# A table of expert products and weights: blocks of two experts by two tokens in place of rows of experts

## The chip, the cores and the metric

The kernel runs on one core of one Trainium2 chip. The metric is the device time of one execution in microseconds (us). TensorE is PE (its weight loads are PEld), VectorE is DVE, ScalarE is ACT, GpSimd is POOL, and SyncE (SP) issues most DMAs.

## The reference, cut to what matters

One transformer-like block on 256 tokens of width 2048: adaLN, a gated MLP and a retention mixer, and then a PEER layer, which is the part that the change touches:

```python
sc = jnp.einsum('thpd,hpnd->thpn', q, subkeys)      # 8 heads, 2 halves, 128 keys
v1, i1 = lax.top_k(sc[:, :, 0], 16); v2, i2 = lax.top_k(sc[:, :, 1], 16)
...                                                 # the 16 best of 16 x 16 sums
eidx = i1 * 128 + i2 (chosen pairs); gate = softmax(top)
a = jnp.einsum('td,thkd->thk', xt, emb_u[eidx])     # 128 chosen experts per token
w = gelu(a) * gate
y = jnp.einsum('thk,thkd->td', w, emb_v[eidx])
```

There are 16,384 experts, 128 chosen for each token.

## The kernel before, in words

The kernel doesn't gather whole expert rows. 768 of the 2048 columns of `emb_u` are gathered by expert (the dots of L762), and for the other 1280 columns PE multiplies **all** experts with all tokens. The results go into one table in SBUF, `A` (L915), of 128 partitions by 128 by 256 fp32 words. An expert is `i1 * 128 + i2`: `n` (the middle index) is `i1`, the partition is `i2`, and `t` is the token. So `A[:, n, t]` lies at word `256 n + t` of a partition: the 256 tokens of one `n` are adjacent, and two neighbours in `n` are 1 KB apart.

Four stages touch `A`:

- **The products** (loop at L919): PE forms 128 x 256 blocks in PSUM (`u_products`), and after every fourth half of an `n` pair ACT copies two `n` at once into `A` (L923, 64 copies of 512 words).
- **The routing stage** (loop at L1024, 32 units of 8 tokens). For a unit, `one_hot` (L948) builds two sets of one-hot matrices, `o1` from `i1` and `o2` from `i2`, on DVE, ACT and POOL (L954, L957, L958, L960); the letters of `ON1`, `ON2`, `ON3` and the counts of `SHARE1`, `SHARE2` say who builds which. `turned` (L965) transposes `o2` on PE (L971) and copies it out of PSUM on ACT (L972). `pick` (L975) multiplies, token by token, the turned `o2` (stationary) with that token's column block of `A` (moving, L981); each of these fp32 products is issued as two passes. DVE then takes the word of the right `n` with one masked sum for each token (`jk`, L985). `weight` (L988) adds the gathered part, applies gelu on ACT (L991) and the gate on DVE (L992). `scatter` (L994) runs two units later: POOL multiplies `o1` by the weights (L997), PE forms the 128 x 128 table of weights of each token (L1001, two passes each), and ACT copies four tokens at a time from PSUM over the picked columns of `A` (L1002). In the first half of the units POOL and DVE also finish the last 16 gathered dots (L755, L762).
- **The second products** (loop at L1137, 128 steps): `v_load(i)` takes row `n = i` of `A`, which now holds weights, splits it into `wh` (ACT, L1075) and `wl` (DVE, L1077), splits the row block of `emb_v` that a DMA brought into `vh` and `vl` (L1079, L1081), and PE accumulates over the steps (L1131). POOL gathers the other 576 columns of `emb_v`, two gathers a step, and DVE adds them (L1064).
- **The end**: `A` is reused as plain memory, `spent` (L1084), for the residual.

Each engine runs its instructions in order, and an instruction of one engine waits for those of others. The calls of `pick`, `turned` and `scatter` are interleaved by hand by unit (`LEAD`, `LAG`, `AHEAD1`); PE's order of a unit is pick, turned of the next unit, scatter of two units back. The number of buffers sets how far an engine runs ahead: three for `o1`, five for `o2`, four for the turned copies.

The lines that read or write the table:

```python
nc.scalar.copy(A[:, n // 2 - 1:n // 2 + 1], sums.pop(n // 4))                      # L923
mm = nc.tensor.matmul(pkv[:, t], oh[:, t], A[:, :, t0 + t], start=True, stop=True)  # L981
put = nc.scalar.copy(A[:, :, t0 + h:t0 + h + 4].rearrange("p n t -> p t n"), pwv)   # L1002
nc.scalar.copy(wh, W[:, i])                                                         # L1075
nc.vector.tensor_tensor(wl, W[:, i], wh.bitcast(F32), op=ALU.subtract)              # L1077
```

Of the kernel before, what the change touches and what calls it, by code (L numbers as in the profile page):

```python
# [10 lines left out]
F32 = mybir.dt.float32  # L11
# [5 lines left out]
ALU = mybir.AluOpType  # L17
# [4 lines left out]
P = 128  # L22
T = 256
# [9 lines left out]
NK = 128  # L33
# [81 lines left out]
def block_kernel(ctx, tc, a, out):  # L115
    nc = tc.nc
    def pool(name, side, bufs=1, space=None):
        stack = ExitStack()
        kw = {} if space == bass.MemoryType.DRAM else {"reuse_waits": "tile"}
        if space is not None:  # L120
            kw["space"] = space
        return stack.enter_context(tc.tile_pool(name=name, bufs=bufs, side=side, **kw)), stack
# [642 lines left out]
    def dot(tt, n, early=False, after=None):  # L765
        if early:
            g = gather(late["pg"], "eg", u_rows, UG, EG, tt, n)
        else:
            g = gather(ph, "hT", u_rows, UG, 8, tt, n, after)
        times(g, tt, n)  # L770
# [106 lines left out]
    def columns():  # L877
        softmax()
        nc.scalar.copy(idr, ident)
        for dst, src in ((i1T, i12[:, 0]), (i2T, i12[:, 1]), (gT, gate)):  # L880
            pt = bank("pt")
            for tt in range(TT):
                nc.tensor.transpose(pt[:, tt * P:(tt + 1) * P], src[:, tt], ident)
            nc.scalar.copy(dst, pt[:, :T])
            if dst is i2T:
                nc.scalar.mul(neg, pt[:, :T], -1.0)
# [4 lines left out]
    sums = {}  # L891

    def u_products(n):
        for m in range(n + len(ready), min(n + 2, 2 * NK)):
            ready.append(u_load(m))
        hi, lo = ready.pop(0)
        first, last = n % 2 == 0, n % 2 == 1
        if n % 4 == 0:
            sums[n // 4] = bank("mmu").rearrange("p (b t) -> p b t", b=2) if n // 4 % 2 else pm.tile([P, 2, T], F32, tag="mm", name="mmu")
        acc = sums[n // 4][:, n // 2 % 2]  # L900
        k0, k1 = HALF[n % 2]
        steps = ((hi, 0), (hi, 1), (lo, 0)) if n >= DIRECT else ((hi, None),)
        for i, (w, part) in enumerate(steps):
            for k in range(k0, k1):
                x = late["x1T"][:, UK + k] if part is None else h2T.op(part, UK + k)
                mm = nc.tensor.matmul(acc, w[:, k - k0], x, start=(first and k == 0 and i == 0),  # L906
                                      stop=(last and k == FK - 1 and i == len(steps) - 1))
        return mm

    for n in range(DIRECT):  # L910
        mm = u_products(n)
    late["pg_s"].close()
    st_s.close()
    big, big_s = pool("big", "left")
    A = big.tile([P, NK, T], F32, tag="big", name="A")  # L915

    rate = (len(todo) - LEFT) / (2 * NK - PRE)
    done = 0
    for n in range(2 * NK):  # L919
        if n >= DIRECT:  # L920
            mm = u_products(n)
        if n % 4 == 3:
            nc.scalar.copy(A[:, n // 2 - 1:n // 2 + 1], sums.pop(n // 4))  # L923
        if n == COLS:
            columns()
        while done < rate * (n + 1 - PRE):
            dot(*todo.pop(0), after=mm)
            done += 1
# [10 lines left out]
    def psum(tag, bufs):  # L939
        b = pq.tile([P, 512], F32, tag=tag, bufs=bufs, name=tag)  # L940
        return b, b.rearrange("p (t n) -> p t n", t=4)
# [33 lines left out]
    def pick(u):  # L975
        for h in range(2):
            t0 = u * SET + 4 * h
            oh = ohs.pop((u, h))
            pk, pkv = psum("pk", 3)
            for t in range(4):  # L980
                mm = nc.tensor.matmul(pkv[:, t], oh[:, t], A[:, :, t0 + t], start=True, stop=True)  # L981
                tc.declare_no_dep(mm.ins, group="scattered", reason="other tokens' columns")
            for t in range(4):
                jk = p2.tile([P, P], F32, tag="jk", bufs=2, name="jk")
                nc.vector.scalar_tensor_tensor(jk, iota, i1T[:, t0 + t:t0 + t + 1], pkv[:, t],  # L985
                                               op0=ALU.is_equal, op1=ALU.mult, accum_out=wT[:, t0 + t:t0 + t + 1])
# [7 lines left out]
    def scatter(u):  # L994
        t0 = u * SET
        o1, o2 = o1s.pop(u), o2s.pop(u)
        nc.gpsimd.tensor_tensor(o1, o1, wT[:, t0:t0 + SET, None].to_broadcast([P, SET, P]), op=ALU.mult)  # L997
        for h in range(0, SET, 4):
            pw, pwv = psum("pw", 3)
            for t in range(4):  # L1000
                nc.tensor.matmul(pwv[:, t], o2[:, h + t].bitcast(F32), o1[:, h + t], start=True, stop=True)  # L1001
            put = nc.scalar.copy(A[:, :, t0 + h:t0 + h + 4].rearrange("p n t -> p t n"), pwv)  # L1002
            tc.add_to_no_dep_group("scattered", put.ins)

    units = T // SET
# [18 lines left out]
    for u in range(-LEAD, units + LAG):  # L1024
        if 0 <= u < units and u % half == 0:
            tt = u // half
            while tt and fetched:
                last_dot()
            pt, _ = psum("pk", 3)
            nc.tensor.transpose(pt[:, :P], wrow[:, tt], ident)  # L1030
            nc.vector.tensor_copy(agT[:, tt * P:(tt + 1) * P], pt[:, :P])
        if 0 <= u < units:
            pick(u)
            weight(u)
        if u + LEAD < units:
            o2s[u + LEAD] = one_hot(1, u + LEAD, (ON2 if u * SET < T // 2 else ON3)[u % 4])
            turned(u + LEAD)
        if 0 <= u < half and fetched and (u + 1) * LEFT > took * half:
            last_dot()
        if u >= LAG:  # L1040
            scatter(u - LAG)
        if 0 <= u + 1 - LAG + AHEAD1 < units:
            v = u + 1 - LAG + AHEAD1
            o1s[v] = one_hot(0, v, ON1[v % 4])
        if 0 <= u < units and u % half == half - 1:
            pt, _ = psum("pk", 3)
            nc.tensor.transpose(pt[:, :P], wT[:, tt * P:(tt + 1) * P], ident)
            nc.vector.tensor_copy(wrow[:, tt], pt[:, :P])
    W = A

    p2_s.close()
    pq_s.close()
    py, py_s = pool("py", "left", bufs=1, space=PSUM)
# [16 lines left out]
    def v_load(i):  # L1070
        room, bufs = (p3, 1) if i % 3 == 2 else (pv, 2)
        vb = room.tile([P, GV], F32, tag="vb", bufs=bufs, name="vb")
        nc.sync.dma_start(vb, v_cols[i * P:(i + 1) * P])
        wh = p3.tile([P, T], F32R, tag="wh", bufs=3, name="wh")
        nc.scalar.copy(wh, W[:, i])  # L1075
        wl = p3.tile([P, T], F32R, tag="wl", bufs=3, name="wl")
        nc.vector.tensor_tensor(wl, W[:, i], wh.bitcast(F32), op=ALU.subtract)  # L1077
        vh = p3.tile([P, GV], F32R, tag="vh", bufs=2, name="vh")
        nc.scalar.copy(vh, vb)  # L1079
        vl = p3.tile([P, GV], F32R, tag="vl", bufs=2, name="vl")  # L1080
        late["split"] = nc.vector.tensor_tensor(vl, vb, vh.bitcast(F32), op=ALU.subtract)  # L1081
        return vh, vl, wh, wl

    spent = A.rearrange("p n t -> p (n t)")  # L1084
    x1 = spent[:, :TT * D].rearrange("p (t d) -> p t d", t=TT)
    xo = spent[:, TT * D:2 * TT * D].rearrange("p (t d) -> p t d", t=TT)
    ga2, gf = spent[:, 4 * D:5 * D], spent[:, 5 * D:6 * D]
# [39 lines left out]
    def product(i, ops, j, tt, n):  # L1127
        vh, vl, wh, wl = ops
        l, r = ((wh, vh), (wl, vh), (wh, vl))[j]
        c, w = chunks[n]  # L1130
        return nc.tensor.matmul(yp[tt][n][:, :w], l[:, tt * P:(tt + 1) * P], r[:, c:c + w],  # L1131
                                start=(i == 0 and j == 0), stop=(i == NK - 1 and j == 2))

    nxt = v_load(0)
    nc.scalar.sqrt(rf, late["ssum"])
    done, rate = 0, len(todo) / (NK - ENDS)
    for i in range(NK - 2):  # L1137
        ops = nxt
        nxt = v_load(i + 1)
        for j in range(3):  # L1140
            for tt in range(TT):
                for n in range(len(chunks)):
                    mm = product(i, ops, j, tt, n)
        while todo and done < rate * (i + 1):
            weigh(*todo.pop(0), after=mm)
            done += 1
        if i == BACK:
            restore(mm)
    ends = [nxt, v_load(NK - 1)]
    for tt in range(TT):  # L1150
        residual(tt, len(parts) - 1)
# [62 lines left out]
```

## Time and profile before

| | us |
|---|---|
| median of 3 runs (2393.7 to 2401.22) | 2394.3 |
| span of the profiled execution, first to last instruction | 2393.9 |
| PE busy | 2208.9 |
| DVE busy | 1785.1 |
| ACT busy | 1031.0 |
| POOL busy | 874.9 |

The profiled execution's span lies 0.4 us under the median. A share of busy time is a mean over stages with different limits, so the stages are read one by one: the routing stage lies from about 1600 to 1804 us of the span, the products before it, the second products after it, to 2365 us.

### The profile page before, as it was taken

How to read it: one execution, taken by the hardware profiler on the slowest of the kernel's cores; microseconds unless marked ns; L12 is line 12 of the kernel's file. 1: busy time of each engine (PE TensorE's matmuls, PEld its weight loads, DVE VectorE, ACT ScalarE, POOL GpSimd, SP SyncE). 2: the span in 40 equal slices, each digit the busy share in tenths (PEclk: the TensorE clock that was granted, in tenths of full speed). 3: DMA queues.
4: the chain of work that ended last, by engine and by line, in shares of the span. 5: the costliest groups of instructions: out<-in, count | busy, mean ns of one | idle time of the engine just before them, and what ended most of it. 6: DMA issues, size and time to landing. Idle time of an engine off the chain costs nothing. (4 is left out here: it accounts for less than half of the span.)

```text
span 2393.9 us, 37307 instructions
## 1 busy us (share of the span) xinstructions
PE 2208.9 (92%) x13988; PEld 1949.2 (81%) x13988; DVE 1785.1 (75%) x3416; ACT 1031.0 (43%) x1440; POOL 874.9 (37%) x750
## 2 busy tenths in 40 slices
PE   6999999999999998893999999989998998998996
PEld 3577779999999888783889999989997777777775
DVE  3478878888788755787767777777766877877777
ACT  3245556643344444101444444457774333333333
POOL 0000000000000002766444444467775665666664
PEclk9999999999999999996999999999999999999998
DMA  9977778777777765767999999971107888888987
GB/s 353 380 296 265 273 267 297 276 286 283 285 295 282 264 213 180 257 224 221 302 302 313 318 316 313 305 248 54 33 1 253 310 301 297 304 306 299 313 310 269
DMA packets 144312, 638.26 MB, mean 267 GB/s; under 512 B 20721, under 2 KB 26625, under 8 KB 112001
## 3 DMA queue, kind: packets, MB, share of 16 engines
q1 hardware_dynamic: 102146, 459.65, 53.7%
q0 software_dynamic: 41984, 176.23, 21.8%
q8 instruction: 109, 1.79, 0.3%
q14 instruction: 73, 0.60, 0.1%
HBM read 631.59 MB, written 4.20 MB: 266 GB/s over the span
## 5 line engine op out<-in xcount | busy, mean ns | idle before, releaser
L755 POOL DMA_INDIRECT gat<-in_peer_v_rows,eidx x256 | 351.4, 1373 | 211.3 <-PE yp L1131 138.7
L755 POOL DMA_INDIRECT gat<-in_peer_u_rows,eidx x256 | 315.0, 1230 | 301.8 <-DVE ulo L710 146.2
L211 ACT CAST whi<-wt 128x2048 fp32r<-128x2048 f32 x130 | 248.0, 1908 | 292.4 <-PE mm L412 224.4
L906 PE MATMUL mmu<-h2T,uhi 128*128 128x256 f32 x2360 | 323.9, 284 | 33.6 <-ACT uhi L709 33.6
L762 DVE SCALAR_TENSOR_TENSOR gat<-gat,h2b 128x768 f32<-128x768 f32 x256 | 245.1, 959 | 142.9 <-DMA gat<-in_peer_u_rows,eidx 141.6
L213 DVE TENSOR_TENSOR wlo<-wt,whi 128x2048 fp32r<-128x2048 f32 (+1 forms) x130 | 292.3, 2249 | 55.5 <-ACT whi L211 51.6
L906 PEld LDWEIGHTS mmu<-h2T,uhi 128*128 128x128 f32 x2360 | 301.8, 193 | 34.4 <-ACT uhi L709 34.4
L1079 ACT CAST vh<-vb 128x1472 fp32r<-128x1472 f32 x128 | 182.9, 1429 | 340.6 <-DMA vb<-in_peer_v_cols 289.4
L356 POOL DMA_DIRECT2D br<-in_b_ada x32 | 15.8, 493 | 773.2 <-DVE ada_acc L357 726.8
L1064 DVE SCALAR_TENSOR_TENSOR yg<-gat,wrow,yg 128x576 f32<-128x576 f32 x254 | 207.5, 817 | 113.0 <-DMA gat<-in_peer_v_rows,eidx 110.8
L709 ACT CAST uhi<-ub 128x640 fp32r<-128x640 f32 x236 | 171.5, 728 | 268.3 <-DMA ub<-in_peer_u_cols 220.8
L1131 PE MATMUL yp<-vl,wh 128*128 128x512 f32 (+1 forms) x768 | 201.3, 396 | 45.9 <-DVE vl L1081 45.0
L353 DVE SCALAR_TENSOR_TENSOR ada_acc<-wa,sc_col,ada_acc 128x256 f32<-128x256 f32 x480 | 231.7, 483 | 11.4
L1081 DVE TENSOR_TENSOR vl<-vb,vh 128x1472 fp32r<-128x1472 f32 x128 | 215.6, 1684 | 6.6 <-ACT vh L1079 6.6
L906 PE MATMUL mmu<-h2T,ulo 128*128 128x256 f32 x1180 | 188.1, 290 | 32.1 <-DVE ulo L710 30.7
L1131 PEld LDWEIGHTS yp<-vl,wh 128*128 128x128 f32 x768 | 139.1, 189 | 96.0 <-DVE vl L1081 72.8
L906 PEld LDWEIGHTS mmu<-h2T,ulo 128*128 128x128 f32 x1180 | 158.2, 192 | 45.8 <-DVE ulo L710 44.7
L1131 PE MATMUL yp<-vh,wh 128*128 128x512 f32 (+1 forms) x768 | 192.2, 384 | 2.6 <-ACT wh L1075 2.6
L710 DVE TENSOR_TENSOR ulo<-ub,uhi 128x640 fp32r<-128x640 f32 x236 | 188.8, 820 | 6.2 <-ACT uhi L709 5.8
L1131 PE MATMUL yp<-vh,wl 128*128 128x512 f32 (+1 forms) x768 | 191.4, 383 | 0.1
L412 PE MATMUL mm<-whi,hT 128*128 128x512 f32 (+1 forms) x832 | 181.7, 362 | 0.0
L1131 PEld LDWEIGHTS yp<-vh,wh 128*128 128x128 f32 x768 | 145.0, 189 | 28.4 <-ACT wh L1075 2.8
(275 smaller groups left out, 3696.2 us busy)
## 6 DMA issues: line engine op xcount, KB each, us to landing
wa<-in_w_ada SPq DMA_DIRECT2D x96, 1024.0 KB
vb<-in_peer_v_cols SPq DMA_DIRECT2D x128, 736.0 KB
ub<-in_peer_u_cols SPq DMA_DIRECT2D x256, 320.0 KB
wt<-in_w_vg SPq DMA_DIRECT2D x32, 1024.0 KB
wt<-in_w_branch_gate SPq DMA_DIRECT2D x32, 1024.0 KB
wt<-in_w_u SPq DMA_DIRECT2D x16, 1024.0 KB
wt<-in_w_b_out SPq DMA_DIRECT2D x16, 1024.0 KB
wt<-in_w_o SPq DMA_DIRECT2D x16, 1024.0 KB
```

The costliest lines, as they stand in the source:

```text
L211: nc.scalar.copy(hi, wt)
L213: nc.vector.tensor_tensor(lo[:, :cut], wt[:, :cut], hi[:, :cut].bitcast(F32), op=ALU.subtract)
L353: nc.vector.scalar_tensor_tensor(acc, wt[:, k], s, acc, op0=ALU.mult, op1=ALU.add)
L412: nc.tensor.matmul(job.ps[b], l, r, start=(first and k == 0 and i == 0 and not lo_part), stop=(last and k == job.rows - 1 and lo_part == 1))
L710: (nc.gpsimd if n < POOL else nc.vector).tensor_tensor(lo[:, :w], ub[:, :w], hi[:, :w].bitcast(F32), op=ALU.subtract)
L755: d = nc.gpsimd.indirect_dma_start(out=g, out_offset=None, in_=table, in_offset=bass.IndirectOffsetOnAxis(ap=rows_of("idx")[:, tt, n:n + 1 ...
L762: nc.vector.scalar_tensor_tensor(g, g, 1.0, h2b[:, tt, :UG], op0=ALU.mult, op1=ALU.mult, accum_out=pe["wrow"][:, tt, n:n + 1])
L906: mm = nc.tensor.matmul(acc, w[:, k - k0], x, start=(first and k == 0 and i == 0), stop=(last and k == FK - 1 and i == len(steps) - 1))
L1064: nc.vector.scalar_tensor_tensor(yg[:, tt], g, w, yg[:, tt], op0=ALU.mult, op1=ALU.add)
L1079: nc.scalar.copy(vh, vb)
L1081: late["split"] = nc.vector.tensor_tensor(vl, vb, vh.bitcast(F32), op=ALU.subtract)
L1131: return nc.tensor.matmul(yp[tt][n][:, :w], l[:, tt * P:(tt + 1) * P], r[:, c:c + w], start=(i == 0 and j == 0), stop=(i == NK - 1 and j = ...
```

## The change

The same words are kept in another order. `A` has five axes: `m` (pair of `n`, 64), `g` (pair of tokens, 128), `b` (which of the two `n`), `s` (which of the two tokens). Word `512 m + 4 g + 2 b + s`. Two `n` by two tokens are 4 adjacent words, 16 bytes. For one token the words of `n` and `n + 1` are 8 bytes apart and the next pair is 2 KB on; for one `n` two tokens are adjacent and the next two are 16 bytes on.

```diff
-    A = big.tile([P, NK, T], F32, tag="big", name="A")
+    A = big.tile([P, NK // 2, T // 2, 2, 2], F32, tag="big", name="A")
+
+    def of_key(n):
+        return A[:, n // 2, :, n % 2, :]
+
+    def of_token(t):
+        return A[:, :, t // 2, :, t % 2]
...
-            nc.scalar.copy(A[:, n // 2 - 1:n // 2 + 1], sums.pop(n // 4))
+            nc.scalar.copy(A[:, n // 4], sums.pop(n // 4).rearrange("p b (g s) -> p g b s", s=2))
...
-                mm = nc.tensor.matmul(pkv[:, t], oh[:, t], A[:, :, t0 + t], start=True, stop=True)
+                mm = nc.tensor.matmul(pkv[:, t].rearrange("p (m b) -> p m b", b=2), oh[:, t], of_token(t0 + t), start=True, stop=True)
...
-            put = nc.scalar.copy(A[:, :, t0 + h:t0 + h + 4].rearrange("p n t -> p t n"), pwv)
+            g0 = (t0 + h) // 2
+            put = nc.scalar.copy(A[:, :, g0:g0 + 2], pwv.rearrange("p (g s) (m b) -> p m g b s", s=2, b=2))
...
-        nc.scalar.copy(wh, W[:, i])
+        w = of_key(i)
+        nc.scalar.copy(wh.rearrange("p (g s) -> p g s", s=2), w)
...
-        nc.vector.tensor_tensor(wl, W[:, i], wh.bitcast(F32), op=ALU.subtract)
+        nc.vector.tensor_tensor(wl.rearrange("p (g s) -> p g s", s=2), w, wh.bitcast(F32).rearrange("p (g s) -> p g s", s=2), op=ALU.subtract)
...
-    spent = A.rearrange("p n t -> p (n t)")
+    spent = A.rearrange("p m g b s -> p (m g b s)")
```

No instruction is added or removed; five groups of instructions get other access patterns. The copy of L1002 wrote single words 1 KB apart and read PSUM in order; in the new form it writes runs of 8 words (two `g` by two `b` by two `s`) and reads PSUM at steps of 128 words.

## Rows read from the trace of the kernel before

**Rows 1.** The page: engines' busy time, and the span in 40 equal slices.
```profile
PE 2208.9 (92%) x13988; PEld 1949.2 (81%) x13988; DVE 1785.1 (75%) x3416; ACT 1031.0 (43%) x1440; POOL 874.9 (37%) x750
...
PE   6999999999999998893999999989998998998996
...
PEclk9999999999999999996999999999999999999998
DMA  9977778777777765767999999971107888888987
```

**Rows 2.** Windows: length, busy us (instructions) by engine, clock, DMA share, GB/s.
```profile
1606.00:1703.00 97.00, 94.71 (x619) 90.06 (x618) 75.21 (x336) 77.01 (x165) 74.35 (x67) 0.98 0.21 61
1703.00:1800.00 97.00, 96.12 (x635) 91.75 (x635) 65.78 (x311) 71.24 (x145) 75.31 (x73) 1.00 0.02 6
...
1900.00:2000.00 100.00, 90.39 (x390) 73.34 (x391) 78.61 (x91) 38.17 (x44) 58.90 (x44) 0.98 0.87 299
```

**Rows 3.** The table's tile: ns min/median/max, first and last start in us.
```profile
L981 PEld LDWEIGHTS pk<-A,oh2T x512: 186/206/338, 1601.6 to 1794.6; 128*128 128x128 f32 x171
...
L1075 ACT CAST wh<-A x128: 388/399/408, 1804.6 to 2364.9; 128x256 fp32r<-128x256 f32 x128
L1077 DVE TENSOR_TENSOR wl<-A,wh x128: 409/418/426, 1806.4 to 2371.5; 128x256 fp32r<-128x256 f32 x128
L923 ACT COPY A<-mmu x64: 572/580/628, 1123.3 to 1596.2; 128x512 f32<-128x512 f32 x64
L1002 ACT COPY A<-pw x64: 1013/1045/1110, 1619.9 to 1802.5; 128x512 f32<-128x512 f32 x64
```

**Rows 4.** Timeline of PE's weight loads in the routing stage: start us, us.
```profile
1619.95 3.37 PEld L981 LDWEIGHTS pk<-A,oh2T 128*128 128x128 f32 x16
...
1674.48 3.36 PEld L981 LDWEIGHTS pk<-A,oh2T 128*128 128x128 f32 x16 [0.20 <-ACT oh2T L972]
...
1713.43 3.36 PEld L981 LDWEIGHTS pk<-A,oh2T 128*128 128x128 f32 x16
...
1755.43 3.38 PEld L981 LDWEIGHTS pk<-A,oh2T 128*128 128x128 f32 x16
1758.82 0.89 PEld L971 LDWEIGHTS pb<-idr,oh 128*128 128x128 f32 x8
1759.66 1.86 PEld L1001 LDWEIGHTS pw<-oh 128*128 128x128 f32 x16
1761.44 2.70 PEld L981 LDWEIGHTS pk<-A,oh2T 128*128 128x128 f32 x13
...
1791.43 3.38 PEld L981 LDWEIGHTS pk<-A,oh2T 128*128 128x128 f32 x16
```

**Rows 5.** Groups by line and form, 1703 to 1800 us, ACT.
```profile
L972 ACT COPY oh2T<-pb 128x512 f32<-128x512 f32 x30 | 16.1, 589 | 18.3 <-PE pb L971 18.3
```

**Rows 6.** Timeline of all engines in the same unit as rows 4.
```profile
1755.81 1.09 DVE L954 TENSOR_TENSOR oh<-kst,colT 128x896 f32<-128x896 f32 x1 [0.79 <-PE pw L1001]
1755.88 3.23 POOL L960 TENSOR_SCALAR oh<-kst,colT 128x128 f32<-128x128 f32 x4 [0.88 <-PE pw L1001]
...
1759.08 1.90 POOL L997 TENSOR_TENSOR oh<-oh,colT 128x1024 f32<-128x1024 f32 x1
...
1761.89 2.96 POOL L960 TENSOR_SCALAR oh<-kst,colT 128x128 f32<-128x128 f32 x4 [0.91 <-PE pw L1001]
```

**Rows 7.** Timeline of POOL, 1640 to 1703 us.
```profile
1656.67 1.55 POOL L960 TENSOR_SCALAR oh<-kst,colT 128x128 f32<-128x128 f32 x2 [1.60 <-PE pw L1001]
1658.39 1.03 POOL L755 DMA_INDIRECT gat<-in_peer_u_rows,eidx  x1 [0.16 <-issue]
1659.44 1.91 POOL L997 TENSOR_TENSOR oh<-oh,colT 128x1024 f32<-128x1024 f32 x1
...
1686.14 2.33 POOL L960 TENSOR_SCALAR oh<-kst,colT 128x128 fp32r<-128x128 f32 x4
```

**Rows 8.** Waits, 1606 to 1703 us: total us, times, longest.
```profile
DVE colT L992 <- ACT colT L991: 7.2, 8, 1.2
```

More of the change, by code (lines that the diff above doesn't have):

```diff
@@ L1048, in block_kernel @@
             nc.vector.tensor_copy(wrow[:, tt], pt[:, :P])
-    W = A
     p2_s.close()
```

## The prediction

> **What bounds the kernel now.** The page comes first: PE is busy 92% of the span, and the slices show it near nine tenths almost everywhere, while the DMA engines fall to 1, 1 and 0 tenths in slices 28 to 30 [rows 1]. So there is one stretch, from about 1600 to 1800 us, in which no transfer can be the limit. [...] PE is the bound and three engines have about a quarter of slack each. The window of the second products is another matter: PE 90.39, DVE 78.61, ACT 38.17 of 100 us with the DMA engines at 0.87 [rows 2].
>
> The timeline then shows what PE does with a unit of eight tokens. Its order is 16 pick passes from 1755.43, 8 transposes from 1758.82, 16 scatter passes from 1759.66, and the next pick at 1761.44 [rows 4]. That is 3.39 + 0.84 + 1.78 = 6.01 us with no gap. A pick pass takes 3.39/16 = 0.212 us and a scatter pass 1.78/16 = 0.111 us, although both load 128 x 128 fp32 weights and stream 128 fp32 columns. The difference that the code shows is the moving operand: the scatter reads adjacent words, the pick reads words 1 KB apart. ACT shows the same cost on a write: the copy of L1002, single words 1 KB apart, takes 1045 ns [rows 3], and the copy of L972, as large and also out of PSUM but written in order, 589 ns [rows 5]. The steps cost 456/512 = 0.89 ns a word on ACT, and (212 - 111)/128 = 0.79 ns a column on PE.
>
> **The change part by part.** *The pick (L981).* It reads two words of one 16-byte block and then jumps 2 KB. No row shows such a read, so it lies between 0.111 us (order) and 0.212 us (a jump at each word). I take 0.111: if a jump costs 0.212 us/128 = 1.65 ns in all, 64 jumps take 0.106 us, which fits into a pass of 0.111. If instead each of 64 jumps adds 0.79 ns, a pass takes 0.162 us. [...] With 0.111 us PE needs 1.78 + 0.84 + 1.78 = 4.40 us for a unit; with 0.162 us 5.21.
>
> *What is late next.* PE doesn't fall to 4.40, since the others have to follow. POOL's busy time is 75.31/16 = 4.71 us a unit in the second half and 74.35/16 = 4.65 in the first; its idle time there is mostly a wait for PE's scatter (0.88, 0.91, 1.60 us) [rows 2, 6, 7]. That time isn't all work that could be pressed closer: four one-hots of L960 take 2.33 us alone [rows 7] and 3.23 us when DVE's L954 of 1.09 us runs beside them, so that one unit's POOL work runs from 1755.88 to 1760.98 without a gap, 5.10 us [rows 6]. [...] DVE has 75.21/16 = 4.70 us a unit in the first half and waits another 7.2/16 = 0.45 us for the gelu of L991, which stands in its order [rows 2, 8]: 5.15. ACT has 77.01/16 = 4.81 and 71.24/16 = 4.45. So about 5.1 us a unit is what POOL and DVE allow, and I take that.
>
> *The copy of L1002.* It writes runs of 32 bytes, so its write is near order; but it reads PSUM at steps of 512 bytes, which no row shows. From 589 ns (neither costs) over 1045 ns (the read costs what the write did) to 1501 ns (twice the 456). Its write comes near the row of L972 and its read is as far out of order as the write of L1002, so neither row is nearer: I take the middle of the two, 0.8 us. ACT then needs 4.81 - 0.49 = 4.3 us in the first half; at 1045 ns it stays at 4.81, still under 5.1; at 1501 ns it needs 5.72 and 5.36 and becomes the bound.
>
> *Copies into the table (L923).* Written in order, read from PSUM as pairs of words. 580 ns now [rows 3], with the same 456 ns as upper end: 64 x 0.46 = 29 us of ACT, spread over the 473 us from 1123 to 1596. ACT was busy 43% of the whole span [rows 1], so I cost it at nothing, but for the last copy, ahead of the first pick: at most 0.5 us.
>
> *The split of weights (L1075, L1077).* 399 and 418 ns for 256 words [rows 3]; pairs of words at steps of 16 bytes. Lower end: as now; upper end 256 x 0.89 = 228 ns more each, 128 x 0.23 = 29 us on each engine. DVE is the nearer one: 78.61% of a step. A step is (2364.9 - 1804.6)/127 = 4.41 us [rows 3], so DVE has 3.47 and would have 3.70. What hides it is DMA at 0.87 and PE at 90%. I take zero; if that cover were thin, a quarter of it, 7 us, could show.
>
> The second products start when the last weights are written, and their 4.41 us a step do not depend on when they start; so what the routing stage gives is kept.
>
> **The sum.** PE-bound pitches: units 3 to 12 (nine, 1619.95 to 1674.48, 54.5 us) and 18 to 31 (thirteen, 1713.43 to 1791.43, 78.0 us) [rows 4]: 132.5 us for 22 pitches, 6.02 each. At 5.1 they take 112.2: **-20.3 us**. Units 12 to 18 take 38.95 us, 6.5 each: PE is not their bound throughout, and I take 0.5 us from each of the six, **-3**. The first three units and the last copies: **-2**. Together -25 against a span of 2393.9; the span is 0.4 us under the median, and the forecast is 2394.3 - 25 = **2369 us**.
>
> **The rivals.** *PE alone sets the pace.* If POOL's and DVE's stretches give way, as they can where L954 falls into POOL's present gap, the pitch is 4.45: 22 x 1.57 = 34.5, 6 x 0.9 = 5.4 and 3, together 43, so 2351 us. For it: POOL's own work is only 2.33 + 1.90 us of a unit when nothing runs beside it. Against it: its gap is where it waits now, and it vanishes.
>
> *The pairs don't help.* The pick stays at 0.212 us, because two words 8 bytes apart are still not adjacent; PE stays the bound, and the cheaper copy of ACT buys nothing: 2394 us. For it: no row shows such a read. Against: the same penalty on ACT and PE, which is what a cost for each place would look like.
>
> *The PSUM read of L1002 makes it slower.* ACT decides once its unit is over 6.02 us: in the first half from (6.02 - 4.81)/2 = 0.60 us more a copy, 1.65 us. At 2.0 us it needs 6.72 and 6.36 us, and 16 x 0.70 + 16 x 0.34 = 17 us are added: 2411 us. [...] For it: each word that the copy reads lies 512 bytes from the last. Against: the copy would have to get three to four times as long as L972's.
>
> **How the numbers follow.** The forecast's case 0.73, PE alone 0.12, no gain 0.08, slower by ACT 0.07. A measurement can tell about 0.3%, 7 us: faster 0.73 + 0.12 = 0.85, same 0.08, slower 0.07. The forecast's own ends: a pick pass of 0.162 us with L1002 unchanged and more waits, a pitch of 5.6: 22 x 0.42 + 1 = 10, so 2384; and the other end reaches to PE alone. The range 2352 to 2385 leaves out the last two cases and the far edge of PE alone.
>
> **What would show it.** Pick passes at about 0.11 us in PE's timeline; the pitch of a unit near 5.1 with POOL's gaps behind L1001 gone and PE idle, waiting for L997, L972 or buffers; L1002 under 1045 ns; wh and wl near 399 and 418 ns; the first wh at about 1779 instead of 1804.6. The forecast is wrong if pick passes stay above 0.16 us, if L1002 is over 1.5 us, or if the step of the second products moves from 4.41 us.

## The result and the profile after

The changed kernel takes 2367.61 us (median of 4 runs, 2360.71 to 2378.43), beside 2395.72 us for the kernel before; the ratio is 0.9887, 95% interval 0.9861 to 0.9913. The forecast was 2369 us, range 2352 to 2385. Two executions of one later experiment, share_none, took 5.6 and 6.1 ms; there is no profile of them, and they are left out of its ratio.

The table's tile in the profile after, with the columns of [rows 3]; the change added lines, so that L981 is now L987, L1002 is L1009, L1075 is L1081 and L1077 is L1083, L923 is L929:

```profile
L987 PEld LDWEIGHTS pk<-A,oh2T x512: 186/188/338, 1603.9 to 1769.4; 128*128 128x128 f32 x171
...
L1081 ACT CAST wh<-A x128: 409/419/436, 1779.1 to 2331.3; 128x256 fp32r<-128x256 f32 x128
L1083 DVE TENSOR_TENSOR wl<-A,wh x128: 409/419/425, 1780.8 to 2335.4; 128x256 fp32r<-128x256 f32 x128
L929 ACT COPY A<-mmu x64: 573/580/632, 1121.3 to 1598.5; 128x512 f32<-128x512 f32 x64
L1009 ACT COPY A<-pw x64: 567/585/609, 1621.0 to 1777.3; 128x512 f32<-128x512 f32 x64
```

The copy of the weights fell from 1045 to 585 ns, the copy of the products stayed at 580, wl at 418 to 419, and wh rose from 399 to 419 ns. The routing stage, counted from the start of the last copy of the products to the start of the first wh, took 1804.6 - 1596.2 = 208.4 us and takes 1779.1 - 1598.5 = 180.6: **27.8 us** less.

PE's weight loads, in the second half of the units (answers to [rows 4]):

```profile
1743.11 1.86 PEld L987 LDWEIGHTS pk<-A,oh2T 128*128 128x128 f32 x16 [0.74 <-ACT oh2T L978]
1744.89 0.77 PEld L977 LDWEIGHTS pb<-idr,oh 128*128 128x128 f32 x8
1745.60 1.86 PEld L1007 LDWEIGHTS pw<-oh 128*128 128x128 f32 x16
1748.19 1.86 PEld L987 LDWEIGHTS pk<-A,oh2T 128*128 128x128 f32 x16 [0.73 <-ACT oh2T L978]
```

Sixteen pick passes and sixteen scatter passes now take the same 1.86 us: the pick has the scatter's rate. The unit shown is 1748.19 - 1743.11 = 5.08 us long, and PE, which had no gap in these units before, waits 0.74 us ahead of its pick. Not every unit is like this one: the next pick comes at 1752.48, after 4.29 us and without a wait; the mean of the thirteen pitches from unit 18 to 31 is 4.99 us. Who holds it, POOL's timeline shows (answers to [rows 6]; L966 was L960, L1003 was L997):

```profile
1737.71 1.89 POOL L1003 TENSOR_TENSOR oh<-oh,colT 128x1024 f32<-128x1024 f32 x1
1739.59 3.25 POOL L966 TENSOR_SCALAR oh<-kst,colT 128x128 f32<-128x128 f32 x4
1742.81 1.89 POOL L1003 TENSOR_TENSOR oh<-oh,colT 128x1024 f32<-128x1024 f32 x1
1744.68 3.11 POOL L966 TENSOR_SCALAR oh<-kst,colT 128x128 f32<-128x128 f32 x4
1747.76 1.89 POOL L1003 TENSOR_TENSOR oh<-oh,colT 128x1024 f32<-128x1024 f32 x1
```

No gap is left: its work of a unit is the unit. The windows say the same, with the columns of [rows 2]:

```profile
1606.00:1687.00 81.00, 69.13 (x565) 66.83 (x565) 76.42 (x312) 62.23 (x151) 72.57 (x60) 0.92 0.21 63
1687.00:1768.00 81.00, 72.56 (x649) 70.08 (x648) 76.85 (x310) 62.18 (x152) 80.41 (x77) 1.00 0.06 20
...
1900.00:2000.00 100.00, 93.33 (x405) 74.17 (x404) 80.37 (x93) 40.41 (x46) 64.69 (x48) 1.00 0.90 312
```

In the second half POOL is busy 80.41 of 81 us; in the first DVE is the fullest, 76.42. Part of DVE's time is instructions that took longer beside POOL's multiplication; these are its one-hots (L954, now L960) in the first half, by line and form, before and after:

```profile
L954 DVE TENSOR_TENSOR oh<-kst,colT 128x896 f32<-128x896 f32 x14 | 15.9, 1134 | 2.0 <-PE pw L1001 1.8
...
L960 DVE TENSOR_TENSOR oh<-kst,colT 128x896 f32<-128x896 f32 x12 | 19.8, 1650 | 2.2 <-PE pw L1007 2.2
```

1650 ns where the same form took 1134 ns beside a POOL that had gaps. Of the twelve, the six that overlap POOL's multiplication took 1.45 to 2.74 us, the six others 1.08 to 1.18. Smaller instructions show it more plainly. The timeline of DVE has the addition of eight words in a row (L990, now L996), in the second half, before and after:

```profile
1725.56 0.15 DVE L990 TENSOR_TENSOR colT<-colT,agT 128x8 f32<-128x8 f32 x1
...
1742.89 1.83 DVE L996 TENSOR_TENSOR colT<-colT,agT 128x8 f32<-128x8 f32 x1
```

The second one begins 0.08 us after POOL's multiplication at 1742.81 and ends with it, at 1744.72 and 1744.70. The sixteen of this half take 760 ns in the mean, where they took 316. Of the sixteen after, the seven that overlap POOL's multiplication end 0.02 to 0.03 us after it, and the nine others take 0.15 or 0.16 us. So a part of DVE's busy time in these windows goes by beside POOL's multiplication and ends only with it.

### The profile page after: what moved, and what is told of

Its sections match the earlier page's. It is cut to its first block, busy times and chain, and to the rows that moved or that the text cites. A ratio compares the mean times of both kernels' runs of the same rounds, so it can differ in the third digit from the quotient of the medians.

```text
span 2359.7 us, 37300 instructions
## 1 busy us (share of the span) xinstructions
PE 2163.8 (92%) x13988; PEld 1905.4 (81%) x13988; DVE 1800.4 (76%) x3416; ACT 1010.4 (43%) x1440; POOL 880.0 (37%) x750
## 5 line engine op out<-in xcount | busy, mean ns | idle before, releaser
L906 PEld LDWEIGHTS mmu<-h2T,uhi 128*128 128x128 f32 x2360 | 302.8, 193 | 34.5 <-ACT uhi L709 33.9
```

## The experiments

Theory A is the prediction's: PE's pick was the bound, and POOL with DVE are the next one. Theory B: the shorter copy of ACT did it. Rival C, for the new bound: PE's own order and the way from pick over DVE and ACT back to PE hold the unit at 5.1 us, whatever POOL does.

### One part alone, or one part undone

**The pick in order, nothing else** (the kernel before; the pick multiplies a constant row in place of the table's column):

```diff
-mm = nc.tensor.matmul(pkv[:, t], oh[:, t], A[:, :, t0 + t], start=True, stop=True)
+mm = nc.tensor.matmul(pkv[:, t], oh[:, t], iota, start=True, stop=True)
```

> The kernel before, with its rows of experts and its copy of L1002 as they were; only the moving operand of the pick is another one: 128 adjacent words of a constant (the row of indices) in place of the token's column of the table, so the weights that come out are not the reference's. Theory A (the gain is PE's: the pick's passes fall from 0.212 to 0.111 us, and POOL with DVE then hold a unit at 5.1 us): passes of 0.111 us, L1002 still 1045 ns, ACT at 4.8 us a unit and just not the bound, a pitch of 5.1 to 5.4 us in the second half, 2366 to 2376 us. Theory B (the shorter copy of ACT is what let the stage go faster): the pitch stays above 5.7 us, 2385 us or more.

Measured: 2367.56 us, ratio 0.9886 (0.9863 to 0.9909): the whole gain. Its copy of the weights and its first wh, in the view of the tile:

```profile
L1075 ACT CAST wh<-A x128: 392/398/408, 1782.4 to 2333.2; 128x256 fp32r<-128x256 f32 x128
...
L923 ACT COPY A<-mmu x64: 575/580/628, 1120.3 to 1600.1; 128x512 f32<-128x512 f32 x64
L1002 ACT COPY A<-pw x64: 1013/1068/1151, 1623.1 to 1780.3; 128x512 f32<-128x512 f32 x64
```

The copy is as slow as it was, and the stage takes 182.3 us all the same.

**The changed kernel with a jump at each word of the pick:**

```diff
-mm = nc.tensor.matmul(pkv[:, t].rearrange("p (m b) -> p m b", b=2), oh[:, t], of_token(t0 + t), start=True, stop=True)
+mm = nc.tensor.matmul(pkv[:, t].rearrange("p (b m) -> p b m", b=2), oh[:, t], of_token(t0 + t).rearrange("p m b -> p b m"), start=True, stop=True)
```

> The changed kernel with the same blocks and the same fast copy; the pick reads the same 128 words of a token in another order: first the 64 even n, then the 64 odd ones, so that each word lies 2 KB from the last and no two follow each other in one block of 16 bytes. The products land in PSUM in that order, so the mask takes another expert's product and the output is not the reference's. Theory A: passes of 0.212 us as before, PE without a gap at 6.0 us a unit, the copy still at 585 ns, 2388 to 2397 us. Theory B: most of the gain stays, 2366 to 2375 us.

Measured: 2388.19 us over 10 runs, ratio 0.9969 (0.9951 to 0.9987). The same blocks in memory, the same words, another order of reading, and most of the gain is gone. First PE's weight loads, then the view of the tile:

```profile
1742.06 3.37 PEld L987 LDWEIGHTS pk<-A,oh2T 128*128 128x128 f32 x16
1748.06 3.36 PEld L987 LDWEIGHTS pk<-A,oh2T 128*128 128x128 f32 x16
```

```profile
L1081 ACT CAST wh<-A x128: 405/420/447, 1796.5 to 2346.9; 128x256 fp32r<-128x256 f32 x128
...
L929 ACT COPY A<-mmu x64: 573/579/632, 1120.4 to 1591.1; 128x512 f32<-128x512 f32 x64
```

Passes of 3.37 us for 16 and a unit of 6.0 us again. The step is now 2 KB and not 1 KB and the passes cost the same, so between these two the distance doesn't count. What both slow reads have, and the fast one hasn't, is that no two words in a row share a block of 16 bytes; a pick of words in neighbouring blocks was not run. The stage takes 1796.5 - 1591.1 = 205.4 us in its profile, 3.0 less than before: the fast copy gives no more than that in this profile, while PE is the bound. The median lies 7.7 us under that of the kernel before; where the rest of it comes from isn't shown.

**The changed kernel with a jump at each word of the copy:**

```diff
-put = nc.scalar.copy(A[:, :, g0:g0 + 2], pwv.rearrange("p (g s) (m b) -> p m g b s", s=2, b=2))
+put = nc.scalar.copy(A[:, :, g0:g0 + 2].rearrange("p m g b s -> p g s b m"), pwv.rearrange("p (g s) (m b) -> p g s b m", s=2, b=2))
```

> The changed kernel, whose copy of the weights into the table goes through the same words in another order: single words 2 KB apart on the write side, steps of two words on the PSUM side. Theory A: the copy takes about 1.0 us again, ACT's busy time in a unit rises by 0.85 us to 4.7, below POOL's 5.1, and the time moves by less than 5 us: 2363 to 2375 us. Theory B: the time goes most of the way back, 2385 us or more.

The row of the table's tile, and then the window of the second half, with the columns of [rows 2]:

```profile
L1009 ACT COPY A<-pw x64: 1013/1057/1130, 1618.6 to 1776.3; 128x512 f32<-128x512 f32 x64
```

```profile
1687.00:1768.00 81.00, 71.90 (x641) 69.39 (x640) 77.76 (x312) 72.64 (x152) 79.22 (x76) 1.00 0.06 19
```

The copy is back at 1057 ns, ACT at 72.64 of 81 us, and POOL is still the fullest. Measured: 2370.24 us, ratio 0.9893 (0.9873 to 0.9913), beside the changed kernel on the same chip:

> The changed kernel once more, as the measure for the others of this chip: 2360 to 2378 us by its four runs; the first operand wh at 1779 us; steps of the second products of 4.35 to 4.45 us.

2368.55 us, 0.9872 (0.9845 to 0.9900); first wh at 1778.5. The intervals overlap: the copy's 1057 - 585 = 472 ns, 64 times, can't be told from nothing. Theory B falls by all three.

### The bound after the change

**Without POOL's multiplication** (the weights don't enter the table):

```diff
-nc.gpsimd.tensor_tensor(o1, o1, wT[:, t0:t0 + SET, None].to_broadcast([P, SET, P]), op=ALU.mult)
```

> The changed kernel without POOL's multiplication of o1 by the weights (L1003, 1.9 us a unit), so the table takes bare one-hots. Theory A (POOL, with DVE through it, holds the unit at 5.1 us): POOL falls to about 2.9 us a unit in the second half, PE becomes the bound or nearly, the pitch there falls to 4.4 to 4.6 us and the stage gives 10 to 18 us: 2350 to 2360 us. Rival C (PE's own order and the way from pick over DVE and ACT to the next transposes hold 5.1 us): the pitch stays at 5.0 to 5.1 us and the time at 2362 to 2370 us.

PE's weight loads in the timeline, and then a window of the second half:

```profile
1744.78 1.87 PEld L987 LDWEIGHTS pk<-A,oh2T 128*128 128x128 f32 x16
...
1749.07 1.87 PEld L987 LDWEIGHTS pk<-A,oh2T 128*128 128x128 f32 x16
...
1753.35 1.87 PEld L987 LDWEIGHTS pk<-A,oh2T 128*128 128x128 f32 x16
```

```profile
1700.00:1760.00 60.00, 60.00 (x563) 60.00 (x562) 52.97 (x279) 50.20 (x126) 39.71 (x50) 1.00 0.01 1
```

The unit is 4.28 us, PE is busy 60.00 of 60 us, and POOL 39.71. With POOL out of the way PE is the bound again, and 4.28 us is what PE needs. So PE's order isn't what holds 5.08. This run also takes the multiplication out of the way from the pick to the scatter, so by itself it doesn't tell POOL's work from that way; the next one does. The time is 2341.81 us over 4 runs (2333.51 to 2361.90), ratio 0.9756 (0.9717 to 0.9794). That is 8 us below the lower end of what was expected, and the stage accounts for it; its tile view, and the picks of units 3 and 12:

```profile
L1081 ACT CAST wh<-A x128: 409/420/435, 1767.1 to 2331.1; 128x256 fp32r<-128x256 f32 x128
...
L929 ACT COPY A<-mmu x64: 576/580/629, 1124.7 to 1612.0; 128x512 f32<-128x512 f32 x64
```

```profile
1632.28 1.86 PEld L987 LDWEIGHTS pk<-A,oh2T 128*128 128x128 f32 x16
...
1673.71 1.86 PEld L987 LDWEIGHTS pk<-A,oh2T 128*128 128x128 f32 x16 [0.64 <-ACT oh2T L978]
```

The stage takes 1767.1 - 1612.0 = 155.1 us, 25.5 less than in the changed kernel, where 10 to 18 were expected. The first half gains too: units 3 to 12 take 41.4 us in place of 47.5. The profiled run is the longest of the four, 2361.90 us, since it loses elsewhere: its last copy of the products starts 13.5 us later than in the changed kernel, and its second products take 564 us from the first wh to the last, against 552.2.

**POOL's share given to ACT and DVE**, a version that leaves nothing out:

```diff
-SHARE1, SHARE2 = (1, 1), (1, 3)
+SHARE1, SHARE2 = (1, 1), (1, 1)
```

> The changed kernel; in the second half POOL builds one of the eight second one-hots of a unit in place of three, ACT or DVE the other two. POOL 1.2 us a unit less (about 3.9), ACT 0.5 more (about 4.3). Theory A: the pitch of the second half falls from 5.1 to 4.5 to 4.7 us, 14 units give 6 to 8 us: 2359 to 2364 us. Rival C: no change, 2366 to 2370 us.

The picks of units 18 and 31:

```profile
1704.03 1.87 PEld L987 LDWEIGHTS pk<-A,oh2T 128*128 128x128 f32 x16
...
1762.35 1.87 PEld L987 LDWEIGHTS pk<-A,oh2T 128*128 128x128 f32 x16
```

The thirteen pitches take 58.3 us in place of 64.9, 4.49 each, with the multiplication and the way from pick to scatter as they were. So in the second half it is POOL's work that held the unit, and rival C falls. Measured: 2357.40 us, ratio 0.9842 (0.9804 to 0.9880), 1.6 us under what was expected. With none of the second one-hots left to POOL in the first half either:

```diff
-SHARE1, SHARE2 = (1, 1), (1, 3)
+SHARE1, SHARE2 = (1, 0), (1, 1)
```

> As share_act, and in the first half POOL builds none of the second one-hots. There DVE is the busier (76 of 81 us). Theory A: the second half as in share_act; in the first half at most 0.3 us a unit, since DVE's sums and gathered dots stay: 2355 to 2363 us. Rival C: no change, 2366 to 2370 us.

Measured: 2351.02 us, 0.9813 (0.9768 to 0.9858), 4 us under what was expected. The changed kernel was not run beside these three, nor beside the first four_by_one below, so share_both was run again beside the changed kernel, and beside a version where POOL builds none of them (`SHARE1, SHARE2 = (1, 0), (1, 0)`):

> The changed kernel beside the next three on one chip: 2360 to 2372 us.

> POOL's share of the second one-hots taken by ACT and DVE, beside the changed kernel on the same chip. Theory A (POOL with DVE was the bound after the change): 10 to 18 us below the changed kernel. If the first difference was the chip's: within 4 us of it.

> POOL builds none of the second one-hots in either half. In share_both the second half ran at 4.3 to 4.9 us a unit, of which PE needs 4.28, so there is little left: 0 to 4 us below share_both, or up to 6 us above it where ACT, with 0.24 us more a unit, comes late with the one-hots for PE's transposes.

On that chip the changed kernel took 2370.96 us (ratio 0.9910, 0.9879 to 0.9941), share_both 2352.84 (0.9835, 0.9807 to 0.9863) and share_none a ratio of 0.9836 (0.9801 to 0.9871). So share_both is **18 us faster than the changed kernel** on one chip, and their intervals don't overlap. Its windows, in the second run, and then the picks of units 3 and 12:

```profile
1606.00:1687.00 81.00, 69.88 (x590) 67.45 (x591) 78.03 (x323) 72.65 (x184) 68.01 (x48) 0.94 0.29 84
1687.00:1755.00 68.00, 66.44 (x605) 65.12 (x604) 62.50 (x295) 64.45 (x168) 58.13 (x46) 1.00 0.06 23
```

```profile
1626.42 1.87 PEld L987 LDWEIGHTS pk<-A,oh2T 128*128 128x128 f32 x16
...
1672.37 1.86 PEld L987 LDWEIGHTS pk<-A,oh2T 128*128 128x128 f32 x16
```

In the second half PE is at 66.44 of 68 us, so there is little more to get from sharing there. share_none gives nothing over it: its units 18 to 31 take 1758.35 - 1696.32 = 62.0 us, where share_both takes 1758.77 - 1700.35 = 58.4. In the first half DVE is at 78.03 of 81. But no run takes work from DVE alone. no_weighting takes work from POOL alone, and share_both moves some of POOL's to ACT and DVE: units 3 to 12 take 41.4 us and 45.95 us in them, against 47.5 in the changed kernel, of which 2.5 us belong to two picks at a granted clock that fell to 0.50 (last section). So POOL is a part of the bound there as well, and that DVE's own work holds the first half isn't shown.

### Two by two, or four by one

Blocks of 16 bytes can also be four experts of one token, so that the pick reads four adjacent words and the row of an expert is single words at steps of 16 bytes (the copies into the table and the splits follow the new order; their lines are left out here):

```diff
-A = big.tile([P, NK // 2, T // 2, 2, 2], F32, tag="big", name="A")
+A = big.tile([P, NK // 4, T, 4], F32, tag="big", name="A")
...
-return A[:, n // 2, :, n % 2, :]
+return A[:, n // 4, :, n % 4]
...
-return A[:, :, t // 2, :, t % 2]
+return A[:, :, t]
```

> The changed kernel with blocks of four experts by one token: the pick reads four adjacent words and jumps, the rows of the second products are single words at steps of 16 bytes. If the cost is one for each new block of 16 bytes: pick passes stay at 0.111 us (two words to a block were enough), wh takes 0.22 + 256 x 1.65 ns = 0.63 us in place of 0.42, wl between 0.42 and 0.65 us; if DVE and PE in the second products have the slack that was read there, the time stays at 2362 to 2372 us; if not, it is up to 2395 us.

```profile
L987 PEld LDWEIGHTS pk<-A,oh2T x512: 186/192/338, 1599.2 to 1765.7; 128*128 128x128 f32 x171
...
L1081 ACT CAST wh<-A x128: 625/652/669, 1775.3 to 2327.6; 128x256 fp32r<-128x256 f32 x128
L1083 DVE TENSOR_TENSOR wl<-A,wh x128: 593/604/630, 1777.1 to 2331.9; 128x256 fp32r<-128x256 f32 x128
```

The pick gains nothing from four words to a block over two: its loads are at 192 ns (188 with two), and the stage takes 1775.3 - 1593.8 = 181.5 us. The reads of the rows do pay: 652 for 419 ns on ACT, 604 for 419 on DVE; the copies of the products, which write two words of a block at a time there, take 622 ns for 580. And the time was 2358.37 us, 0.9841 (0.9805 to 0.9877), not above the changed kernel's in its other runs but below it, and under the 2362 to 2372 us expected. Run again beside that one:

> Blocks of four experts by one token once more, since the first run came out at 2358 us, below the changed kernel's 2368 us on another chip. If the routing stage and the second products are what sets the time, both are as in the changed kernel (first wh 181 us after the last copy of the products, steps of 4.35 us), and the two agree within 4 us. If the two-by-two blocks cost something that was not seen, this one is 6 to 12 us faster again.

2362.59 us (2359.97 to 2365.34), 0.9885 (0.9859 to 0.9912), against 2370.96 (2361.16 to 2375.81). The stage is the same, 1778.0 - 1596.6 = 181.4 us against 1779.8 - 1597.8 = 182.0. The rest is in the second products: 2330.9 - 1778.0 = 552.9 us from first to last wh, against 559.9. But the changed kernel itself had 552.2 and 557.2 us there in its two other profiles, so this stretch varies by as much from run to run. The expectation had put 6 to 12 us on a cost of the two-by-two blocks that was not seen, and the medians differ by 8.4; but the two ratios' intervals overlap, and no stage shows such a cost. Whether slower splits make the second products steadier stays open too. What is shown is that 233 ns of ACT and 185 ns of DVE in each of 128 steps, 30 and 24 us in all, cost nothing.

## Why the prediction was right

The picks of units 3, 12, 18 and 31 after the change, on which two of the readings below rest:

```profile
1621.59 1.87 PEld L987 LDWEIGHTS pk<-A,oh2T 128*128 128x128 f32 x16
...
1669.04 1.87 PEld L987 LDWEIGHTS pk<-A,oh2T 128*128 128x128 f32 x16
...
1702.89 1.87 PEld L987 LDWEIGHTS pk<-A,oh2T 128*128 128x128 f32 x16
...
1767.74 1.87 PEld L987 LDWEIGHTS pk<-A,oh2T 128*128 128x128 f32 x16
```

- **The pass of the pick.** Taken at 0.111 us; it is (1.86 - 0.19)/15 = 0.111. The middle value of 0.162 us, with a cost added at each jump, is excluded. That 64 jumps of 1.65 ns, an estimate from the slow pass, fit into a pass agrees with this: at two words to a block the pass has the scatter's rate (1.86 us for 16), and four words add nothing (loads of 192 ns, 188 with two).
- **The pitch.** Taken at 5.1 us over 22 PE-bound pitches, -20.3 us. Units 3 to 12 now take 1669.04 - 1621.59 = 47.45 us, 5.27 each, and 18 to 31 take 1767.74 - 1702.89 = 64.85 us, 4.99 each; together 112.3 us for 132.5, **-20.2**. That the sum is met to 0.1 us is luck: at 5.1 a unit the second half came out 1.45 us shorter than taken, the first 1.55 us longer. For the second half the reason given, POOL without a gap, is in the windows, and no_weighting and share_act show that it is the reason. For the first half the windows show DVE nearly without a gap, but the runs show POOL as a part of that bound, and DVE alone was not tested.
- **Units 12 to 18.** Taken at -3; 1702.89 - 1669.04 = 33.85 us for 38.95, -5.1. PE was the bound there more than I allowed: pick_in_order, with the old copy, takes 1704.98 - 1671.05 = 33.9 us for the same units.
- **Start and end.** Taken at -2; 2.5 of the 27.8 us lie ahead of unit 3 and behind the last pick.
- **The copy of L1002.** Taken at 0.8 us; it is 0.585, the lower end: reading PSUM at steps of 512 bytes cost ACT nothing here. The size was off by 0.2 us and decided nothing, as copy_jumps shows. The rival that ends slower rested on this read and is out.
- **The split of weights.** Taken at zero; wh is 20 ns longer. An estimate from other rows gives about that: a word costs ACT (580 - 399)/256 = 0.71 ns (the 580 ns read PSUM, the 399 ns SBUF), and 128 blocks at PE's 1.65 ns take 211 ns where 256 words take 182, 29 ns more. That this is the cause isn't shown. The cover held: not even the far end of the range, which four_by_one about reaches, costs time.
- **The second products.** 552.2 us from first to last wh where they were 560.3, a step of 4.35 us for 4.41, which the prediction had named as a sign against it. This is not the change's doing, since the old layout with the fast pick had 550.8 and the changed kernel 557.2 and 559.9 in other runs. So of the 34 us between the two profiled spans only 28 belong to the change, which is also what the medians differ by.

For reads by PE the runs show 3.37 us for 16 passes with no two words in a row in one block of 16 bytes ([rows 4] and pick_jumps), and 1.86 with two. For POOL beside DVE the rows show that four one-hots take 2.33 us where DVE's begins only with the last of them [rows 7], and 3.25 where it runs beside them. How much of the new pace this is, no run separates.

## What to carry to other kernels

PE read fp32 words one by one across rows here (3.37 us for 16 passes), and ACT wrote them so (1045 ns for 512 words). With two of the words in each direction in a block of 16 bytes the column cost PE as little as the scatter's adjacent words (1.86 us) and ACT 585 ns, and the row cost hardly more than before (419 ns for 399 on ACT, 419 for 418 on DVE). In a table that is used in both directions such a layout is worth a run. When the engine that bounds a stage is made faster, the next bound is found by taking the busy time of the others and asking which of their instructions took longer beside another engine's; here that gave 5.1 us a unit (4.99 and 5.27 measured), and shifting the sharing afterwards gave another 18 us. A cheaper instruction on an engine that was not the bound (the copy, 460 ns for 64 times) made no difference by itself that copy_jumps could tell.

## What the runs showed of the hardware that was not expected

- **PE's clock fell where PE had got gaps.** The granted clock of the first half of the changed kernel is 0.92, where it was 0.98 before [rows 2]. Among units 3 to 12 two of the 16-pass picks take over 3 us in place of 1.87, each soon after a wait of PE for POOL or ACT; first the timeline of PE's weight loads, then the windows around them, with the clock as third number from the end:

```profile
1630.43 2.17 PEld L1007 LDWEIGHTS pw<-oh 128*128 128x128 f32 x16 [2.00 <-POOL oh L1003]
1632.48 3.23 PEld L987 LDWEIGHTS pk<-A,oh2T 128*128 128x128 f32 x16
...
1661.10 0.74 PEld L977 LDWEIGHTS pb<-idr,oh 128*128 128x128 f32 x8 [1.93 <-ACT oh L964]
...
1663.56 3.05 PEld L987 LDWEIGHTS pk<-A,oh2T 128*128 128x128 f32 x16
```

```profile
1630.00:1640.00 10.00, 9.56 (x72) 9.56 (x73) 10.00 (x39) 7.05 (x19) 9.32 (x9) 0.83 0.06 25
...
1660.00:1670.00 10.00, 8.89 (x68) 8.90 (x69) 9.50 (x42) 8.10 (x19) 7.48 (x7) 0.83 0.13 40
```

  In stretches of 1 us the granted clock is 0.50 from 1632 to 1635 us and from 1663 to 1666, and 0.82 to 0.98 in the ones next to them. The two picks are 1.36 and 1.18 us longer, 2.5 us together; the nine pitches missed the forecast by 9 x 0.17 = 1.5 us. So of what the faster picks gave, these two gave 2.5 us back. Not each wait did this: ahead of the second products PE waits 2.50 us for ACT's wh, at 1779.6, and the clock stays at 1.00 (1779 to 1783 us). That a wait is the reason isn't shown.
- **ACT read PSUM at steps of 512 bytes as fast as in order**: 585 ns for 512 words, 589 in order [rows 5]; on the SBUF side single words at far steps cost 1045 with PSUM read in order [rows 3] and 1057 in copy_jumps.
- **DVE paid too**: 604 ns in place of 419 for 256 words, when each lay in another block of 16 bytes (four_by_one).
- **A small DVE instruction took about as long as POOL's large one beside it**: the addition of eight words in a row took 1.83 us beside POOL's multiplication of 1.89, and 0.15 us without it.
